# Loading the first contraction slice of b in four pieces in place of two

## The chip, the cores and the metric

The kernel runs on one core of a Trainium2 chip. The metric is the device time of one execution in microseconds, given as the median of several runs. A core has TensorE (PE, matrix products into PSUM), VectorE (DVE), ScalarE (ACT), GpSimd (POOL) and SyncE (SP), which here only issues transfers. Transfers between the device memory and the on-chip memory are carried out by 16 DMA engines; SP and POOL issue them from queues of their own.

## The reference

With a of 1024 x 1024, b of 1024 x 2048 and c of 2048 x 1024, all float32:

```python
def reference(a, b, c):
    h = np.matmul(a, b)
    h = 0.5 * h * (1 + np.tanh(np.sqrt(2 / np.pi) * (h + 0.044715 * h ** 3)))
    return np.matmul(h, c).astype(np.float32)
```

## The kernel before, in words

The kernel computes h transposed, applies the activation while it moves h out of PSUM, and multiplies by c. Both products use seven half-size block products in place of eight for part of the work (class `Seven`, function `seven`): the columns 1024 to 2047 of the first product, and the whole of the second product. The columns 0 to 1023 of the first product are done plainly, in the stretch that the change touches.

**The first stage.** The contraction of the first product has 1024 rows, cut into eight slices of 128 (KT = 8, KH = 4). For the first half of the rows of a (512 rows) and slices 0 to 3, the inputs come as float32 through staging buffers: `sta` for a, `stb` for b (columns 0 to 1023 of each slice). SP issues these loads in the order written (lines 76 to 83): slice 0 of a, slice 0 of b, slice 1 of a, slice 1 of b, slices 2 and 3 of a in one, slice 2 of b, slice 3 of b. `load_a` (L71) and `load_b` (L74) issue one transfer each.

For every slice `turn0` casts a to bf16 (VectorE, L118), transposes it on TensorE (L122) into PSUM, and copies it to `aT` (VectorE, L124). For b, ScalarE casts columns 0 to 511 (L135) and VectorE columns 512 to 1023 (L136) into `b1`. For slice 0 ScalarE's cast is cut in two of 256 columns, in the kernel before already. Then seven matmuls of 128 x 512 (L128), one per tile of 128 columns of b and each into its own PSUM bank, accumulate slice k. The first two tiles need columns 0 to 255 of the slice, the next two 256 to 511, the last three 512 and up. Eight matmuls on zeros (L89) run while the first loads are on their way.

**What follows.** POOL issues all other loads; these convert float32 to bf16 on the way. They stand behind one small copy, the gate (L85), which reads slice 1 of b in `stb` and so waits for its landing. After the gate come four loads of a (L98, the second half of its rows), slices 4 to 7 of b (L105), two more loads of a, the rest of b (L109) and c (L112). After slice 3, TensorE transposes the second half of a's rows (`turn`, L158) from what L98 loaded. The order on each engine is that of the code, since the schedule is written by hand.

**Completion of transfers.** SP's transfers rotate over eight completion semaphores: the ninth uses that of the first again, and its issue waits until the first has landed. In the kernel before SP issues eight loads and then sixteen stores of the output (L353).

These are the lines that cast b in the first stage:

```python
    for k in range(KH):
        for c0 in (0, 256) if k == 0 else (0,):
            w = 256 if k == 0 else H
            nc.scalar.activation(b1[:, k, ds(c0, w)], stb[:, k, ds(c0, w)], AF.Copy)
        nc.vector.tensor_copy(b1[:, k, H:], stb[:, k, H:])
```

Of the kernel before, what the change touches and what calls it, by code (L numbers as in the profile page):

```python
# [19 lines left out]
def kernel(ctx, tc, a, b, c, out):  # L20
# [4 lines left out]
    H = 512  # L25
# [44 lines left out]
    def load_a(k, n):  # L70
        nc.sync.dma_start(out=slice_a(k, n), in_=av[:, 0:4, ds(k * 128, n * 128)])  # L71

    def load_b(k, c0=0, w=1024):
        nc.sync.dma_start(out=stb[:, k, ds(c0, w)], in_=bv[:, k, ds(c0, w)])  # L74

    load_a(0, 1)
    load_b(0, 0, H)
    load_b(0, H, H)
    load_a(1, 1)
    load_b(1)  # L80
    load_a(2, 2)
# [330 lines left out]
```

## Time and profile before

| | |
|---|---|
| median of 8 runs | 122.38 us |
| lowest and highest | 121.48 and 124.96 us |
| the profiled execution | 121.48 us |
| its span in the profile | 119.7 us |
| TensorE busy | 112.4 us, 94% of the span |
| VectorE busy | 88.6 us, 74% |
| ScalarE busy | 50.8 us, 42% |
| bytes read and written | 20.97 MB and 4.19 MB |

The span is the time between the first and the last event of the profile; what the device time has beyond it, 1.8 us here, lies around it. The profile shows one execution. Times in it are microseconds from the start of the span. Engine names end in q where the sequencer of an engine is meant, as in SPq for SP's issues. A group of instructions is given by its line and engine, what it writes and reads, its shapes and its count, followed by its busy time, the mean length of one, and the idle time of the engine in front of it with what ended that idle time. In the list of waits the numbers after a pair are the microseconds in total, how often it occurred, and the longest.

### The profile page before, as it was taken

How to read it: one execution, taken by the hardware profiler on the slowest of the kernel's cores; microseconds unless marked ns; L12 is line 12 of the kernel's file. 1: busy time of each engine (PE TensorE's matmuls, PEld its weight loads, DVE VectorE, ACT ScalarE, POOL GpSimd, SP SyncE). 2: the span in 40 equal slices, each digit the busy share in tenths (PEclk: the TensorE clock that was granted, in tenths of full speed). 3: DMA queues.
4: the chain of work that ended last, by engine and by line, in shares of the span. 5: the costliest groups of instructions: out<-in, count | busy, mean ns of one | idle time of the engine just before them, and what ended most of it. 6: DMA issues, size and time to landing. Idle time of an engine off the chain costs nothing.

```text
span 119.7 us, 1429 instructions
## 1 busy us (share of the span) xinstructions
PE 112.4 (94%) x530; PEld 72.2 (60%) x536; DVE 88.6 (74%) x97; ACT 50.8 (42%) x82; POOL 16.3 (14%) x29
## 2 busy tenths in 40 slices
PE   6788899999999999999999999999999999999970
PEld 2234454645544445888887444468888888888850
DVE  0224488496438899987779999969999996892480
ACT  4022471007457789946769436900023595100000
POOL 2008908842242000000000000000000000000000
PEclk9999999999999999999999999999999999999999
DMA  3799999999999999998000000072000002004695
GB/s 95 175 364 394 177 169 213 206 202 206 206 207 212 210 213 212 209 210 159 8 0 0 0 5 0 0 263 88 0 0 0 0 5 88 0 0 175 246 351 192
DMA packets 11110, 16.34 MB, mean 136 GB/s; under 512 B 736, under 2 KB 5856, under 8 KB 11104
## 3 DMA queue, kind: packets, MB, share of 16 engines
q0 software_dynamic: 6496, 8.91, 42.5%
q1 hardware_dynamic: 4608, 7.34, 17.5%
q8 instruction: 4, 0.07, 0.2%
q14 instruction: 2, 0.02, 0.0%
HBM read 20.97 MB, written 4.19 MB: 210 GB/s over the span
## 4 chain that ended last, share of the span: by engine, by line
PE 78%; DMA 9%; DVE 7%; issue 1%; ACT 1%; SPq 0%; DVEq 0%; ACTq 0%
PE ps L229 51%; PE ps L128 25%; DMA out_dram<-ot 5%; DMA stb<-in_b_dram 4%; DVE x L187 4%; PE pt L158 2%; DVE ot L273 2%; PE pt L122 1%; DVE aT L124 1%; DVE ot L358 1%; ACT u L268 1%; ACT b L135 0%; SPq L71 0%; DVEq L273 0%; DVEq L358 0%
## 5 line engine op out<-in xcount | busy, mean ns | idle before, releaser
L128 PE MATMUL ps<-aT,b 128*128 128x512 bf16 x125 | 30.1, 393 | 2.0 <-DVE aT L124 1.0
L229 PE MATMUL ps<-x,s 128*128 128x512 f32 x128 | 29.6, 391 | 0.0
L229 PEld LDWEIGHTS ps<-x,s 128*128 128x128 f32 x128 | 24.0, 188 | 5.1
L128 PEld LDWEIGHTS <-b 128*128 128x128 bf16 x128 | 12.5, 100 | 16.5 <-ACT b L135 2.2
L229 PE MATMUL ps<-x,x 128*128 128x512 f32 x64 | 14.8, 389 | 0.0
L229 PE MATMUL ps<-c_sb,hT 128*128 128x512 bf16 x62 | 13.9, 379 | 0.1
L229 PEld LDWEIGHTS ps<-x,x 128*128 128x128 f32 x64 | 12.0, 188 | 2.5
L268 ACT ACTIVATE v<-ps 128x512 f32<-128x512 f32 x8 | 4.8, 599 | 17.1 <-PE ps L229 17.1
L163 ACT ACTIVATE hT<-ps 128x512 bf16<-128x512 f32 x12 | 6.8, 594 | 11.3 <-PE ps L128 11.3
L229 PE MATMUL ps<-x 128*128 128x512 f32 x48 | 11.3, 393 | 0.0
L229 PEld LDWEIGHTS <-hT 128*128 128x128 bf16 x64 | 6.2, 98 | 7.6 <-issue 0.3
L229 PEld LDWEIGHTS ps<-x 128*128 128x128 f32 x48 | 9.0, 188 | 2.0
L187 DVE TENSOR_TENSOR x<-c_sb 128x1024 fp32r<-128x1024 bf16 x8 | 9.2, 1216 | 0.0
L273 DVE TENSOR_TENSOR ot<-ps,v 128x512 f32<-128x512 f32 x8 | 5.3, 686 | 4.6 <-DMA out_dram<-ot 3.8
L258 DVE TENSOR_TENSOR half<-ps,half 128x512 f32<-128x512 f32 x8 | 5.5, 692 | 3.2 <-PE ps L128 2.9
L273 DVE TENSOR_TENSOR ot<-ps,u 128x512 f32<-128x512 f32 x8 | 5.4, 690 | 3.0 <-ACT u L268 3.0
L160 DVE COPY aT<-pt 128x1024 bf16<-128x1024 bf16 x6 | 4.0, 688 | 4.7 <-PE pt L158 4.7
L163 ACT ACTIVATE hT<-ot 128x512 bf16<-128x512 f32 x12 | 6.9, 624 | 1.1 <-DVE ot L273 1.1
L112 POOL DMA_DIRECT2D c_sb<-in_c_dram x8 | 5.7, 714 | 10.0 <-DMA b<-in_b_dram 9.1
L229 PE MATMUL ps<-aT,b 128*128 128x512 bf16 x31 | 7.0, 379 | 0.1
L268 ACT ACTIVATE p<-ps 128x512 f32<-128x512 f32 x8 | 4.7, 594 | 4.8 <-PE ps L229 4.8
L135 ACT ACTIVATE b<-stb 128x512 bf16<-128x512 f32 (+1 forms) x5 | 2.6, 541 | 9.2 <-DMA stb<-in_b_dram 9.2
(45 smaller groups left out, 115.1 us busy)
## 6 DMA issues: line engine op xcount, KB each, us to landing
c_sb<-in_c_dram POOLq DMA_DIRECT2D x8, 512.0 KB, 19.7
out_dram<-ot SPq DMA_DIRECT2D x16, 256.0 KB, 2.1
b<-in_b_dram POOLq DMA_DIRECT2D x4, 512.0 KB, 12.8
stb<-in_b_dram SPq DMA_DIRECT2D x3, 512.0 KB, 8.4
a<-in_a_dram POOLq DMA_DIRECT2D x6, 256.0 KB, 7.3
b<-in_b_dram POOLq DMA_DIRECT2D x4, 256.0 KB, 9.0
sta<-in_a_dram SPq DMA_DIRECT2D x2, 256.0 KB, 4.3
stb<-in_b_dram SPq DMA_DIRECT2D x2, 256.0 KB, 5.0
```

Source lines behind the costliest of these rows:

```text
L112: nc.gpsimd.dma_start(out=c_sb[:, t:t + 2], in_=cv[:, t:t + 2])
L122: nc.tensor.transpose(pt[:, i, ts(j, 128)], ab[:, j, ts(i, 128)], ident)
L128: nc.tensor.matmul(p, b1[:, k, ts(t, 128)], aT[:, h, k], start=(k == k0), stop=(k == k1 - 1))
L135: nc.scalar.activation(b1[:, k, ds(c0, w)], stb[:, k, ds(c0, w)], AF.Copy)
L158: nc.tensor.transpose(pt[:, n, ts(j, 128)], sts[j // 2][:, j % 2, ts((k + n) % KH, 128)], ident)
L160: nc.vector.tensor_copy(aT[:, h, k:k + 2], pt)
L163: nc.scalar.activation(hT[h][:, t], p, AF.Gelu_apprx_tanh)
L187: nc.vector.tensor_tensor(out=dst[:, r], in0=x[:, r], in1=y[:, r], op=op)
L229: nc.tensor.matmul(p[:, ds(c0, w)], l[:, k, ts(j, 128)], r[:, k, ds(c0, w)], start=(start and k == 0), stop=(k == self.kt - 1), skip_group ...
L258: nc.vector.tensor_tensor(out=half[:, t], in0=p, in1=half[:, t], op=ADD)
L268: nc.scalar.activation(st, p, AF.Copy)
L273: nc.vector.tensor_tensor(out=ot, in0=p, in1=st, op=ADD)
```

## The change

The first slice of b, 128 rows by 1024 columns of float32, is loaded by four transfers of 256 columns each. Before, it was two of 512. Nothing else in the text of the kernel changes; the casts that read the slice are the same.

```diff
     load_a(0, 1)
-    load_b(0, 0, H)
-    load_b(0, H, H)
+    for c0 in range(0, 1024, 256):
+        load_b(0, c0, 256)
     load_a(1, 1)
     load_b(1)
     load_a(2, 2)
```

SP now issues ten loads ahead of its stores, and each transfer of slice 0 moves rows of 1024 bytes where it moved rows of 2048. ScalarE's two casts of slice 0 each wait for a transfer of their own, where both waited for the first; VectorE's cast of columns 512 to 1023 waits for two transfers in place of one. On SP the issue of slice 2 of b now waits for the semaphore of slice 0 of a, and that of slice 3 for the first piece of slice 0 of b.

## The prediction

> **What bounds the kernel now.** I read the chain that ended last first, in order of time, because the change sits in the first five microseconds and the question is whether they are on the path. Columns: start us, length us, what.
>
> ```profile
> 1.22 4.66 DMA stb<-in_b_dram
> 5.90 0.43 ACT b L135
> 6.37 3.17 PE ps L128 x7
> 9.54 0.44 PE pt L122 x4
> 10.01 0.44 DVE aT L124
> 10.48 1.67 PE ps L128 x7
> ...
> 16.30 0.11 PE pt L158 x2
> 16.41 0.01 issue
> 16.42 0.51 PE pt L158 x6
> ```
>
> The first piece of b, issued at 1.22, lands at 5.88 and holds the first real matmul until 6.37. From there TensorE or what feeds it is on the path to 101.4. But the first matmul has another condition. The timeline of 4 to 7 us and the groups by shape (6 to 10 us, then 10 to 16 us) show it:
>
> ```profile
> 5.55 0.42 DVE L124 COPY aT<-pt 128x512 bf16<-128x512 bf16 x1 [1.65 <-PE pt L122]
> 5.90 0.72 ACT L135 ACTIVATE b<-stb 128x256 bf16<-128x256 f32 x2 [3.67 <-DMA stb<-in_b_dram]
> ```
> ```profile
> L128 PE MATMUL ps<-aT,b 128*128 128x512 bf16 x7 | 3.2, 630 | 0.9 <-ACT b L135 0.9
> L128 PE MATMUL ps<-aT,b 128*128 128x512 bf16 x20 | 4.8, 378 | 1.1 <-DVE aT L124 1.0
> ```
>
> aT is written at 5.97-5.99, so whatever b does, the first matmul can't start before about 6.03: 0.34 us of 6.37. And the first seven matmuls run at 630 ns (0.43 us apart), later ones at 378 (0.21 apart), although the granted clock reads 1.00.
>
> Then the list of waits between 6 and 17 us, and the same stretch in windows (PE, PEld, DVE, ACT, POOL busy, clock, DMA share, GB/s):
>
> ```profile
> ACT b L135 <- DMA stb<-in_b_dram: 9.2, 4, 3.7
> POOL gate L85 <- DMA stb<-in_b_dram: 8.1, 1, 8.1
> PEld L158 <- DMA a<-in_a_dram: 0.2, 1, 0.2
> ```
> ```profile
> 2.00:3.00 1.00, 1.00 (x4) 0.43 (x3) 0.00 (x0) 0.22 (x2) 0.00 (x0) 1.00 0.88 271
> 3.50:5.00 1.50, 1.35 (x6) 0.25 (x4) 0.40 (x1) 0.00 (x0) 0.00 (x0) 1.00 0.38 67
> 6.00:8.00 2.00, 1.63 (x4) 0.54 (x5) 0.43 (x1) 0.62 (x2) 0.00 (x0) 1.00 1.04 359
> 10.00:12.00 2.00, 1.52 (x8) 0.78 (x9) 1.46 (x3) 0.04 (x1) 2.00 (x4) 1.00 1.01 392
> ```
>
> Two things are to be seen. The small wait of 0.2 us at L158 is the second checkpoint: TensorE arrives at 16.30 and cannot go on past 16.41 until the second POOL load of a has landed (16.38). That load is issued behind the gate, which waits for b's slice 1 (landed 9.39), and shares 16 busy DMA engines. So an earlier first matmul is worth nothing at the end unless this landing comes earlier too; a later landing costs in full. After it I found no load nearer than 1.1 us to its user (b's slice 7 lands at 25.02, its first matmul comes at about 26.1). Second, the DMA engines have a hole, 67 GB/s between 3.5 and 5.0, just after b is first touched; from 6 on they are full.
>
> **What the Trainium skill says.** *DMA: Bandwidth & Descriptors*, "Issuing engines are not separate DMA queues": all transfers share the same 16 engines; "HWDGE ordering" adds that each engine takes its descriptors in ring order. The trace agrees: SP's loads land in their order, 3.45, 5.88, 7.17, 8.04, 9.39, 10.83, 12.10, 13.36. The same page, "Why small descriptors are slow", gives a fixed cost of some 3 cycles a packet; the trace's packet records have 84 ns for 2048 bytes and 46 for 1024, so 8 ns lost per split, which agrees. *TensorE: Matmul & The Clock Gate*, Part 1: the array runs at half rate until a free-running window of about 3.4 us has been busy, and the moment varies from run to run. The 630 against 378 ns agree; the varying moment can't be seen in one trace.
>
> **The change, step by step**, against the profiled execution's own 121.48 us (span 119.7 and 1.8 outside it). The median of the runs is 122.38, 0.9 above it; I carry differences over.
>
> 1. SP issues two more loads. The issue timeline:
> ```profile
> 1.22 0.97 SPq L74 DMA_DIRECT2D stb<-in_b_dram  x2
> 2.23 0.43 SPq L71 DMA_DIRECT2D sta<-in_a_dram  x1
> 2.70 0.50 SPq L74 DMA_DIRECT2D stb<-in_b_dram  x1
> ```
> An issue is 0.48 us, so the four pieces go out at 1.22, 1.70, 2.19, 2.67, and all that follows on SP (a1, b1, a2, b2, b3) goes out 0.97 later: a1 at 3.20, b1 3.67, a2 4.2, b2 4.7, b3 5.6. From the issue of the first load (0.74) to its first packet (1.84) the trace has 1.1 us, so a1 could start at 4.3. In the trace its first packets move at 5.5 and it lands at 8.04. The delay is hidden by the queue ahead of it, cover about 1.2 us; without the cover it costs up to 0.97. POOL's queue is untouched, apart from its gate.
> 2. New waits on SP. The program rotates eight completion semaphores; with ten loads, b2 now waits for a0's landing (3.45, before its issue, nothing) and b3 for the first piece (at most 5.9, against its own issue at 5.6, so 0.3 at most). Behind b3 on SP stand only the stores, the first of them after 68 us. b3's packets move after 11 us. Cost nothing. The stores keep their distance of eight.
> 3. Packets. Each engine carries 32 of 46 ns in place of 16 of 84: 1.47 against 1.34, +0.13 us of DMA work, in front of everything that lands later, so the gate and the POOL load at the checkpoint move by +0.13.
> 4. First piece. Half the bytes: 8 x 46 = 0.37 us per engine in place of 0.67, so 0.3 earlier if the hole stays where it is; how the hole falls on it the trace can't say. Bounds: 4.5 (no hole) to 5.9 (all of it). I take 5.4. ACT 0.43 later, 5.85, TensorE is held by aT: first matmul at 6.03, -0.34 (0 if it lands at 5.9).
> 5. VectorE's cast of columns 512 up (L136) now waits for two landings, 7.17 + 0.13, done 7.75; its weights are wanted at 6.03 + 4 x 0.43 = 7.75. Cost 0 to 0.1. ACT's second half waits for its own piece, wanted at 6.89; hidden unless that lands after 6.4.
> 6. Going on: transposes of slice 1 at 9.26 (9.54 before), aT at 10.17; ACT on b1 from 9.54, done 10.17, matmuls at 10.20 (10.48). Slice 2: transposes 11.87, aT 12.80, but ACT on b2 runs 12.25-12.88, matmuls at 12.93 (13.12). TensorE is thus 0.19 early, and reaches the checkpoint at 16.11. The load lands at 16.51 instead of 16.38, and TensorE goes on at 16.55 instead of 16.42.
>
> Sum: -0.34 at the first matmul, eaten on the way; +0.13 at the checkpoint: 121.6 in the profile's terms, 122.5 in the median's. The hole in the DMA could move by itself: below nothing if smaller pieces fill it (up to 1.0 us of the 1.5 are idle), above if more transfers widen it. And in the typical run, 0.9 longer than the profiled one, TensorE may be later than the load, and then the 0.2 to 0.3 us survive. Between +0.13 and -0.3 I take no change, **122.4**.
>
> **The rivals.**
>
> *Slower: the later issues are not hidden.* If b's pieces go through without the hole, or the engines must wait for each transfer's descriptors, a1, b1, a2, b2, b3 begin by their issue times, 0.97 later, and with them the gate and the checkpoint load. For it: several DMA engines stand idle between 3.6 and 5.0 us although the second half was issued by 2.19. Against: 1.2 us of queue ahead of a1. It decides once the queue ahead of a1 is under 0.97 us at its issue. Time: 122.38 + 0.97 = 123.35; half of it, 122.9.
>
> *Faster: TensorE's full rate comes earlier in the typical run.* The idle gap before the first matmul shrinks from 0.86 to 0.52 us; if that brings the clock release forward, seven matmuls at half rate cost 7 x 0.21 = 1.5 less, of which the loads leave about 0.9, the median falling to what the profiled run already is: 121.5. Against: the profiled run ran all of slice 0 at half rate and yet is the shortest, so in such a run nothing more is to be had.
>
> *The DMA hole closes.* The transfers come up to 1.0 us earlier; TensorE's own chain then caps the gain at 0.34: 122.0. This stays within the unmeasurable.
>
> *Nothing happens at the first matmul*, since the first piece takes the whole hole and lands at 5.9: then only +0.13, 122.5.
>
> **How the numbers follow.** About 0.5% (0.6 us) is what a measurement of this kernel can tell from no change. My forecast with the last two rivals, all between 121.8 and 123.0: 0.51. Faster beyond that: 0.26, the clock rival with some cases where both clock and hole move. Slower: 0.23, the issue rival and a widened hole. The range reaches to the clock rival's 121.5 and a little further and to 123.2, most of the issue rival, so that a tenth lies outside at either end.
>
> **What would show it.** SP's issues: a1 near 3.2. The landing of the first b piece: before 5.5, with the first matmul at 6.03 behind aT, shows step 4 right; at 5.9, wrong. The second POOL load of a at L158: landing 16.4 to 16.6 with a wait of 0.4 us in front of it shows steps 3 and 6 right. Wrong would be: a1 landing near 9 with DMA engines idle before it (issue rival); a landing at L158 well before 16.3 (hole closed); or matmuls of slice 0 at 378 ns (clock rival).

## The result

The changed kernel takes 123.82 us in the median of 11 runs (122.84 to 124.7; a twelfth on record took 122.6); the kernel before, 122.33 over 32 runs. The ratio is 1.0133, with a 95% interval of 1.0103 to 1.0162: slower by 1.3%, about 1.5 us. Ratios leave out executions more than 1.5% above the fastest of their kernel; both kernels have such. Run again on another occasion, in four executions, the change gave 1.0156 (1.0087 to 1.0225). The forecast of no change was wrong, and its range ended at 123.2.

The profiled execution took 123.76 us, with a span of 122.0. Its chain of waits, in order of time (start, length, what), to be held against the chain of before:

```profile
3.18 0.43 SPq L71
...
3.65 6.74 DMA stb<-in_b_dram
...
10.42 0.64 ACT b L135
...
11.10 2.56 PE ps L128 x7
13.66 0.87 PE pt L122 x8
...
15.03 2.59 PE ps L128 x11
...
18.27 0.45 PE pt L158 x8
```

The chain no longer goes through the first piece of b, but through slice 1 of b: issued at 3.65 (2.70 before), landed at 10.40 (9.39 before). Slice 1's matmuls begin at 11.10 in place of 10.48, and then last 2.56 in place of 1.67 us.

The timeline of TensorE in the changed kernel shows that slice 0 had gone the other way:

```profile
5.83 1.74 PE L128 MATMUL ps<-aT,b 128*128 128x512 bf16 x7 [0.51 <-ACT b L135]
7.46 0.40 PE L122 MATMUL pt<-ident,ab 128*128 128x128 bf16 x4
11.10 2.56 PE L128 MATMUL ps<-aT,b 128*128 128x512 bf16 x7 [3.25 <-ACT b L135]
```

The first matmul comes 0.54 us earlier and in this execution at full rate. TensorE is through with slice 0 and the transposes by 7.86, and then idles for 3.25 us. The gain of the first stage is there, and is wiped out by the wait that follows.

The windows of the changed kernel (length, then busy time of PE, PEld, DVE, ACT, POOL, granted clock, DMA share, GB/s):

```profile
3.50:5.00 1.50, 1.35 (x6) 0.25 (x4) 0.35 (x1) 0.42 (x1) 0.00 (x0) 1.00 0.72 195
6.00:8.50 2.50, 1.85 (x11) 0.63 (x9) 1.28 (x3) 0.00 (x0) 0.00 (x0) 1.00 0.81 215
12.00:15.00 3.00, 2.52 (x12) 1.35 (x11) 1.34 (x3) 1.20 (x2) 3.00 (x6) 0.50 0.97 187
```

The kernel before has 362 GB/s in the second of these windows:

```profile
6.00:8.50 2.50, 2.13 (x6) 0.71 (x7) 0.85 (x2) 0.62 (x2) 0.00 (x0) 1.00 1.04 362
```

Two things have changed. The hole in the DMA traffic, which stood between 3.5 and 5.0 us at 67 GB/s, is shallower there (195) but there is a second one from 6.0 to 8.5, while slice 1 of b is on its way. And between 12 and 15 us TensorE's granted clock is 0.50, which lengthens the matmuls of slice 1 and the transposes behind them. TensorE comes to the transposes of L158 at 18.27, where it came at 16.30 before and went on, after a short wait, at 16.42; from there on the order of its work is the same.

A third thing has changed at the other end of the kernel. This is the issue of SP's last store, first in the kernel before, then in the changed one:

```profile
116.81 0.33 SPq L353 DMA_DIRECT2D out_dram<-ot  x1
```
```profile
118.67 0.33 SPq L353 DMA_DIRECT2D out_dram<-ot  x1
```

The stores land at 118.83 and 120.73, and the spans end at 119.71 and 121.99. From the last landing to the end it is thus 0.89 us before and 1.25 us after the change. The trace shows the reason. At its end SP waits for the completion semaphores one after the other, in a fixed order and 0.06 us apart. With 24 transfers the rotation puts the last store on the semaphore that comes last in this order; with 26 it puts it on an earlier one, and six more waits follow its landing. In the twenty profiles of this case this rest goes by the number of loads from SP and ScalarE alone: 0.89 to 0.90 us with eight, 1.25 to 1.26 with ten, 1.32 with nine, 0.95 or 0.96 with seven. So 0.36 us of the loss have nothing to do with the head of the kernel; no run changed this end alone.

### The profile page after: what moved, and what is told of

The parts are those of the page before. It is cut to its first block, busy times and chain, and to the rows that moved or that the text cites. A ratio compares the mean times of both kernels' runs of the same rounds, so it can differ in the third digit from the quotient of the medians.

```text
span 122.0 us, 1432 instructions
## 1 busy us (share of the span) xinstructions
PE 111.8 (92%) x530; PEld 72.0 (59%) x536; DVE 89.0 (73%) x97; ACT 50.9 (42%) x82; POOL 16.5 (14%) x29
## 3 DMA queue, kind: packets, MB, share of 16 engines
q0 software_dynamic: 6496, 8.91, 41.9%
## 4 chain that ended last, share of the span: by engine, by line
PE 75%; DMA 11%; DVE 6%; SPq 2%; issue 1%; ACT 1%; DVEq 0%; ACTq 0%
PE ps L229 50%; PE ps L128 22%; DMA stb<-in_b_dram 6%; DMA out_dram<-ot 5%; DVE x L187 4%; PE pt L158 2%; DVE ot L273 2%; SPq L74 1%; PE pt L122 1%; SPq L71 1%; DVE ot L358 1%; ACT b L135 1%; ACT u L268 0%; DVE aT L124 0%; DVEq L273 0%
## 5 line engine op out<-in xcount | busy, mean ns | idle before, releaser
L128 PE MATMUL ps<-aT,b 128*128 128x512 bf16 x125 | 29.6, 388 | 4.4 <-ACT b L135 3.8
L229 PE MATMUL ps<-aT,b 128*128 128x512 bf16 x31 | 7.0, 379 | 0.1
```

Source lines behind the costliest of these rows:

```text
L128: nc.tensor.matmul(p, b1[:, k, ts(t, 128)], aT[:, h, k], start=(k == k0), stop=(k == k1 - 1))
L229: nc.tensor.matmul(p[:, ds(c0, w)], l[:, k, ts(j, 128)], r[:, k, ds(c0, w)], start=(start and k == 0), stop=(k == self.kt - 1), skip_group ...
```

## The experiments

Theory 1: the loss comes from the later issues on SP. Everything behind slice 0 of b is issued 0.95 us later and lands later. Theory 2: it comes from the smaller pieces, which upset the transfers. Beside these, the half rate of TensorE between 12 and 15 us: cause, or part, or nothing. The 0.36 us at the end are in every kernel here that has ten loads.

### Issues without pieces: two tiny loads

The tile `tiny` is allocated further up.

```diff
     load_b(0, 0, H)
     load_b(0, H, H)
+    for i in range(2):
+        nc.sync.dma_start(out=tiny[:, ds(4 * i, 4)], in_=bv[:, 0, ds(4 * i, 4)])
```

> b's slice 0 stays in two loads of 512 columns; two loads of 16 bytes a row stand behind them on SP, so that only the number of issues is that of the change (the tiny tile is read by nothing). Theory 1, later issues: slice 1 of a is issued near 3.2 us in place of 2.2, slice 1 of b near 3.65, it lands near 10.4 (9.4 before), and most of the loss of the change comes back: +1.0 us or more, ratio 1.008 to 1.014. Theory 2, the smaller pieces themselves: no loss, ratio 1.000 to 1.003, slice 1 of b lands near 9.4 to 9.6 though it is issued later.

Ratio 1.0112 (1.0041 to 1.0182). SP's issues in the timeline of this kernel, and the gate, which starts 0.05 after the landing of slice 1:

```profile
2.23 0.91 SPq L81 DMA_DIRECT2D tiny<-in_b_dram  x2
3.17 0.43 SPq L72 DMA_DIRECT2D sta<-in_a_dram  x1
3.65 0.51 SPq L75 DMA_DIRECT2D stb<-in_b_dram  x1
```
```profile
10.88 0.44 POOL L88 COPY gate<-stb 128x1 f32<-128x1 f32 x1 [9.59 <-DMA stb<-in_b_dram]
```

Slice 1 of b is issued at 3.65, as after the change, and lands at 10.83, later still, though slice 0 comes in two pieces. Two issues that carry 16 bytes a row cost most of what the change costs. This is with the 0.36 us at the end, and with a mean granted clock of 0.977 to 0.983 in all its four executions.

### Pieces without issues: two of the four on ScalarE's queue

`load_b` takes the issuing engine as a further argument here.

```diff
     for c0 in range(0, 1024, 256):
-        load_b(0, c0, 256)
+        load_b(0, c0, 256, nc.sync if c0 < H else nc.scalar)
```

> The four pieces of the change, with the last two issued by ScalarE at the start of its program, so that SP issues what it issued before. Theory 1: slice 1 of b is issued near 2.7 and lands near 9.4; the loss of the change goes, ratio 0.995 to 1.003. Theory 2: it lands near 10.4 as after the change, ratio 1.008 to 1.014.

Ratio 0.9978 (0.9946 to 1.0011). SP's issue timeline and the gate:

```profile
2.26 0.43 SPq L71 DMA_DIRECT2D sta<-in_a_dram  x1
2.74 0.51 SPq L74 DMA_DIRECT2D stb<-in_b_dram  x1
```
```profile
9.32 0.18 POOL L85 COPY gate<-stb 128x1 f32<-128x1 f32 x1 [8.02 <-DMA stb<-in_b_dram]
```

Ten loads, four small pieces, and no loss, although the end has its 0.36 us here too: slice 1 of b is issued at 2.74 and lands at 9.27. The order of the loads is another one as well: the two pieces on ScalarE's queue go out at 0.74 and 1.19, slice 0 of a lands at 5.42 (3.45 before), and the first matmul comes at 6.84. With this reserve the two experiments together speak for theory 1 and against theory 2 as the main cause.

### Time alone: SP held

What counts could be the clock time of the issues, or the two more transfers in SP's queue.

```diff
     load_b(0, 0, H)
     load_b(0, H, H)
+    nc.vector.memset(sta[:, ds(H, 1920)], 0.0)
     load_a(1, 1)
```

> The kernel before, with no transfer added or cut: SP is held ahead of the issue of slice 1 of a until VectorE has cleared the part of the staging buffer that it writes, to about 2.9 to 3.2 us in place of 2.2. Theory 1a, the time of issue is what counts: all landings behind come 0.7 to 1.0 us later (slice 1 of b near 10.1 to 10.4), ratio 1.006 to 1.014. Theory 1b, it is the two more transfers in SP's queue and not the clock time of the issues: slice 1 of b lands near 9.4, ratio 0.998 to 1.003.

Ratio 1.0062 (1.0031 to 1.0093). SP's timeline, the gate, and the window of the second hole:

```profile
3.17 0.38 SPq L71 DMA_DIRECT2D sta<-in_a_dram  x1
3.59 0.51 SPq L74 DMA_DIRECT2D stb<-in_b_dram  x1
```
```profile
10.96 0.44 POOL L86 COPY gate<-stb 128x1 f32<-128x1 f32 x1 [9.66 <-DMA stb<-in_b_dram]
```
```profile
6.00:8.50 2.50, 2.46 (x6) 0.89 (x7) 0.85 (x2) 0.29 (x1) 0.00 (x0) 1.00 0.89 184
```

The same eight loads with the same sizes, only 0.9 us later from slice 1 of a on: slice 1 of b lands at 10.90, and the second hole is there, 184 GB/s. The delay alone makes the late landing. It makes only half of the loss in time; with its eight loads this kernel does not have the 0.36 us at the end.

### Is the early landing of before the rule?

The profile of before was that of the shortest execution of its first eight. Three more profiles of it and one of the changed kernel, on one chip:

> The kernel before, looked at again. Theory 1a rests on slice 1 of b landing near 9.4 in one profiled execution, the shortest of its set; 256 and 768 columns landed it at 9.55 and at 10.35 with the same issue times. If the earlier landing is the rule, it lies within 9.2 to 9.7; if the issue time only shifts the odds between an early and a late landing, one or two of the three looks show 10.0 or later.

> As the look before it: slice 1 of b at 9.2 to 9.7 if the early landing is the rule, at 10.0 or later in some looks if the issue time shifts the odds.

> The third look at the kernel before: again 9.2 to 9.7 if the early landing is the rule, 10.0 or later in some looks if the issue time shifts the odds.

> The changed kernel, looked at beside the three of the kernel before: slice 1 of b lands at 10.3 to 10.8 again, as in all four executions seen so far.

The kernel before took 121.88, 121.71 and 121.68 us; slice 1 of b landed at 9.23, 9.14 and 9.28. The changed kernel took 122.97 and landed it at 10.52. With the profiles shown first (9.39 and 10.40) and a third of the changed kernel (10.49, below) the shift is 1.0 to 1.4 us in every pair. It belongs to every execution profiled, not to one. In this profile of the changed kernel TensorE ran slice 0 at half rate as in the first profile of before, and slice 1 at full rate:

```profile
6.04 3.14 PE L128 MATMUL ps<-aT,b 128*128 128x512 bf16 x7 [0.52 <-DVE aT L124]
11.23 1.68 PE L128 MATMUL ps<-aT,b 128*128 128x512 bf16 x7 [1.62 <-ACT b L135]
14.21 3.18 PE L128 MATMUL ps<-aT,b 128*128 128x512 bf16 x13 [0.52 <-DVE aT L124]
17.23 0.68 PE L158 MATMUL pt<-ident,a 128*128 128x128 bf16 x8
```

Without the half rate in slice 1 it is 1.1 to 1.3 us longer than the three beside it (one execution each). Of this, 0.36 us lie at the end. Behind the transposes of L158 TensorE goes on with its matmuls at 17.75, against 16.93 to 17.10 in the three: in these executions the late landings by themselves cost these 0.65 to 0.82 us. Slices 2 and 3 of a, whose transposes follow, landed at 12.00, against 10.6 to 10.7 in the three. In the first of those TensorE comes to L158 at 15.80 and waits there for the second POOL load of a, which sets the end as the prediction read it from the trace of before:

```profile
15.80 0.27 PE L158 MATMUL pt<-ident,a 128*128 128x128 bf16 x2
16.75 0.51 PE L158 MATMUL pt<-ident,a 128*128 128x128 bf16 x6 [0.68 <-DMA a<-in_a_dram]
```

In the changed kernel's execution beside it both conditions are met almost at once: TensorE comes at 17.23, and the second POOL load, behind its later gate, lands at 17.36.

### The half rate

> The changed kernel again, as the measure for the others of this group. Theory 1a: slice 1 of b is issued near 3.65 and lands near 10.4 again; ratio 1.010 to 1.016. If that landing was an accident of one execution, it lands near 9.5 this time.

The changed kernel again: 123.94 us, ratio 1.0156, slice 1 of b at 10.49, half rate from 11.9 to 15.4.

```diff
         if k < 2:
             turn0(k + 1, k + 1)
+        if k == 0:
+            fill = bank(7, name="fill")
+            for _ in range(10):
+                nc.tensor.matmul(fill, warm[:, 0:128], warm, start=True, stop=True)
```

> The change, with ten matmuls on zeros behind the transposes of slice 1, while TensorE waits for slice 1 of b. Their results are read by nothing. Theory 1 says nothing of the clock: slice 1 of b lands near 10.4 as after the change. If TensorE's half rate between 11.7 and 15.3 us is a part of the loss, the granted clock reads 1.0 there, the seven matmuls of slice 1 take 1.7 in place of 2.6 us, and the ratio falls to 1.005 to 1.009. If the clock is without effect: ratio 1.012 to 1.015 as after the change.

> The changed kernel with four matmuls on zeros (read by nothing) behind the transposes of slice 1. If half rate in the gap before slice 1 is a part of the loss, the time lies 0.3 to 0.7 us under that of the changed kernel of this group, ratio 1.004 to 1.010; if the clock has no part in it, within 0.2 us of it. Slice 1 of b lands near 10.4 in either case.

With ten fills, as in the lines above: ratio 1.0068 (1.0031 to 1.0104), slice 1 of b at 10.35 as expected. The interval touches that of the change, which begins at 1.0103. The 14 of 20 executions that are in the ratio all have a granted clock of 0.99 or more over their span; of the six left out, at 124.1 to 125.9 us, five have 0.985 or 0.986. Its profile, though, is of an execution with slice 0 at half rate, where the fills themselves delayed slice 1:

```profile
6.03 3.15 PE L128 MATMUL ps<-aT,b 128*128 128x512 bf16 x7 [0.51 <-DVE aT L124]
10.17 2.32 PE L144 MATMUL fill<-warm 128*128 128x512 bf16 x10 [0.52 <-DVE aT L124]
12.32 1.68 PE L128 MATMUL ps<-aT,b 128*128 128x512 bf16 x7
```

With four fills nothing was gained, 1.0148 (1.0044 to 1.0253). Four were too few to hold the rate, so this kernel doesn't test the question:

```profile
8.57 1.02 PE L144 MATMUL fill<-warm 128*128 128x512 bf16 x4 [0.52 <-DVE aT L124]
11.46 2.87 PE L128 MATMUL ps<-aT,b 128*128 128x512 bf16 x7 [1.87 <-ACT b L135]
```

The unaltered kernels give a second reading. Of 14 executions of the changed kernel that are in the ratios, 9 have a mean granted clock under 0.988 and a median of 123.95 us; the other 5 have 123.17. Of 112 of the kernel before, 8 lie under 0.988, with 123.0, and 104 above, with 122.2. So a low clock goes with some 0.8 us in either kernel, and the changed kernel has it much more often. Two reserves belong to this. The same split gives 1.0 us with two pieces on ScalarE's queue and 0.7 with SP held, but nothing with 256 and 768 columns or with a on ScalarE's queue (both below). And the record of the clock begins only when full rate is first granted: at 9.96 us in the first profile of before, at 4.94 in that of the changed kernel. Half rate ahead of this moment is not in the mean, so the executions above 0.988 are not free of it: eleven of the thirteen that were profiled ran slice 0 at half rate.

When the rate is lost again can be read from the traces. After the first grant the clock changes only in steps of 3.41 us. In seven profiles a step at full rate is followed by one at half rate while matmuls are still to come; in it TensorE was busy for 0.42 to 1.58 of the 3.41 us. In all other steps at full rate ahead of the last matmuls, some 600 in the twenty profiles, it was busy for 1.72 us or more, about half of the step, and full rate went on. These are the windows of such a step in the first and in the second profile of the changed kernel:

```profile
8.35:11.77 3.42, 0.67 (x4) 0.32 (x5) 0.43 (x1) 0.63 (x1) 1.32 (x3) 1.00 1.03 386
```
```profile
10.04:13.46 3.42, 2.06 (x14) 0.99 (x15) 1.39 (x3) 0.80 (x2) 2.88 (x5) 1.00 0.98 321
```

In the first, granted full rate early, the wait for slice 1 of b fills most of a step, and half rate follows at 11.77. In the second, granted it at 10.04, no step has so much idle time. With four fills the step has 1.36 busy us, still too few. So it is the share of busy time in a step that goes with the loss, and with it the moment of the first grant. This is read from the profiles without an exception; no run changed the idle time alone.

### Other numbers of loads

```diff
-    load_b(0, 0, H)
-    load_b(0, H, H)
+    load_b(0, 0, 256)
+    load_b(0, 256, 256)
+    load_b(0, H, H)
```

> Three pieces, of 256, 256 and 512 columns: one issue more than before. Theory 1: half the loss, slice 1 of b issued near 3.2 and landing near 9.9, ratio 1.003 to 1.008. If a loss comes only with the fourth piece: 0.998 to 1.002.

Ratio 1.0105 (1.0041 to 1.0169), more than half of the loss, and not by the expected way: in the one profile (122.97 us) slice 1 of b was issued at 3.18 and landed at 8.95, earlier than before. There the loss came at the second checkpoint, as the list of waits from 14 to 19 us has it:

```profile
PEld L159 <- DMA a<-in_a_dram: 1.5, 1, 1.5
```

The second POOL load of a landed at 17.40 in place of 16.4 to 16.7. Why it was late in that execution stays open. With nine loads the end takes 0.43 us more than before, which is a third of this loss.

```diff
-    load_b(0, 0, H)
-    load_b(0, H, H)
+    load_b(0, 0, 256)
+    load_b(0, 256, 768)
```

> Two loads again, but of 256 and 768 columns, so no issue is added. Theory 1: slice 1 of b lands near 9.4 as before; the ratio is 0.997 to 1.002, since the second load of a at L158 still holds the end. Theory 2, a small first piece upsets the transfers behind it: slice 1 of b lands near 10.4, ratio 1.008 to 1.014.

> 256 and 768 columns again, since three of its four executions were disturbed the first time. Theory 1a: no issue is added, slice 1 of b lands near 9.4 to 9.6, ratio 0.997 to 1.003. If a small first piece does harm by itself: 1.006 to 1.014.

> 256 and 768 columns, a third look. Slice 1 of b landed at 9.55 and at 10.35 with the issue times of before. Theory 1a alone gives 9.2 to 9.6. 10 or later again would mean that a small first piece delays the landings by itself, and that the added issues are not the only cause of the loss.

The first set of four executions, three of them at 125.3 to 125.6 us, gives no ratio. The second gave 1.0054 (1.0020 to 1.0088). In the three profiles, the first of them of an execution of 125.45 us, slice 1 of b landed at 9.55, 10.35 and 10.00, though it was issued at 2.7. A small first piece with a large second one therefore costs something without any added issue, about 0.6 us (0.2 to 1.1 by the interval); theory 1 doesn't account for that.

```diff
-    load_b(0, 0, H)
-    load_b(0, H, H)
+    load_b(0)
```

> One load of 1024 columns for slice 0 of b: one issue less than before, slice 1 of b issued near 2.2. Theory 1a with the floor that the bytes set (9.2 us with the loads of a on ScalarE's queue): slice 1 of b lands between 8.9 and 9.5, no later than before; the first matmul waits until about 7.1, and the ratio is 0.997 to 1.005. If few, large loads were what speeds up the landings beyond the time of issue: slice 1 of b lands by 8.6, ratio under 0.997.

> One load of 1024 columns for slice 0 of b, again. Its first look (an execution of 122.4 us, while most of its runs took 121.4 to 122.0) had slice 1 of b at 10.33, against the 8.9 to 9.5 that theory 1a gives for an issue at 2.2. If that look was untypical: 8.9 to 9.5 now. If landings go by something else than the issue times: 10 or later again. Ratio 0.993 to 0.999 in either case.

One load is faster than the kernel before: 0.9959 (0.9929 to 0.9990), and 0.9964 (0.9941 to 0.9987) in a second set, by 0.4%. In the first profile slice 1 of b landed at 10.33 against the expectation, in the second at 8.91, in line with it. The chain of the second has no transfer in it at all up to 17.7 us:

```profile
1.19 3.61 PE warmps L88 x8
...
6.04 3.17 PE ps L127 x7
...
10.14 1.67 PE ps L127 x7
...
15.96 0.45 PE pt L157 x8
```

The whole slice landed at 5.54, before the second half of the kernel before did (6.6 to 7.2), and the first matmul waits only for aT. This version beats both kernels.

### Two other orders

```diff
-        nc.sync.dma_start(out=slice_a(k, n), in_=av[:, 0:4, ds(k * 128, n * 128)])
+        nc.scalar.dma_start(out=slice_a(k, n), in_=av[:, 0:4, ds(k * 128, n * 128)])
```

> The kernel before, with the three loads of a issued by ScalarE at the start of its program, so that SP issues slice 1 of b near 1.7 in place of 2.7 us. Theory 1a: landings follow the issues as far as the engines can carry the bytes; slice 1 of b lands by 8.6 to 9.0, and the second load of a at L158 with it; ratio 0.990 to 0.998. If the landings are held by the bytes alone, slice 1 of b lands at 9.3 or later and the ratio is 0.998 to 1.006.

Ratio 1.0091 (1.0068 to 1.0114). Slice 1 of b, issued at 1.66, landed at 9.17, no earlier than before; slice 0 of a, now sharing the DMA engines with b from the start, landed at 6.04 (3.45 before), and slices 2 and 3 of a at 12.90 (10.83). An issue a microsecond earlier brought nothing here; that the bytes ahead then hold the landing is the likely reading (387 GB/s from 6.0 to 8.5 us, no hole), but with a on another queue the order of those bytes changed too.

```diff
-    load_a(1, 1)
-    load_b(1)
+    load_b(1)
+    load_a(1, 1)
```

> The change, with slice 1 of b issued ahead of slice 1 of a, near 3.2 in place of 3.65 us. Theory 1a: slice 1 of b lands near 9.9, its gate opens 0.5 earlier than after the change; slice 1 of a lands later, by 8.5 to 9.5, which the transposes can bear; ratio 1.004 to 1.011. If the time of issue is not what counts: as after the change, 1.011 to 1.016.

On top of the change: 1.0104 (0.9986 to 1.0221), which settles nothing; in the one profile, of an execution of 125.68 us, slice 1 of b landed at 9.42, slice 1 of a only at 10.37, and that now held TensorE.

## Why the prediction was wrong

**Step 1, the later issues, failed.** Their times were right: slice 1 of a at 3.18 (3.20 forecast), slice 1 of b at 3.65 (3.67). That the delay is "hidden by the queue ahead of it, cover about 1.2 us" was wrong. The cover was worked out from the first load, 1.1 us from issue to first packet, and from slice 1 of a alone. Slice 1 of a did come through, at 6.95, 8.18 and 8.32 in three profiles against 7.4 to 8.0 in the four of before. It was the next load that paid: slice 1 of b takes 6.4 to 6.7 us from issue to landing in the kernel before and 6.7 to 6.9 in the changed one, so that 0.95 us of later issue became 1.0 to 1.4 us of later landing. Holding SP alone moved the landing by 1.5 to 1.8. Half the delay did not: issued at 3.18, slice 1 of b landed at 8.95 with three pieces, and at 9.42 with four where slice 1 of a stood behind it. Slices 2 and 3 of a and slice 2 of b follow at 11.88 and 13.15 in place of 10.83 and 12.10, again 1.05 later.

**Step 2, the waits on SP, was right at the head and wrong at the end.** Slices 2 and 3 of b were issued at 4.68 and 5.23, without a wait to be seen. But the step put the stores behind them at nothing, since they "keep their distance of eight". They do; the two more loads move the last store to another semaphore, and that costs 0.36 us.

**Step 3, packets, +0.13 us,** is not to be seen on its own beside 1 us. The 8 ns lost per split agree with the three cycles cited there in kind, not in size: by the step's own figures 32 bytes take about 1.2 ns (38 ns for 1024 bytes), so that three cycles, at the 32 bytes a cycle of the example in the section that it cites, would be an estimated 3.6 ns, less than half of what was measured.

**Step 4, the first piece, was right and useless.** It landed at 4.38 (4.41 and 3.99 in the two other profiles), below the lower bound of 4.5 and 1 us before the 5.4 taken; the first matmul came at 5.83, 6.04 and 5.90 (6.03 forecast). Note that in one of the four profiles of the kernel before it came at 6.07 as well. Step 5 cost nothing: the last piece landed at 6.17, ahead of the 7.30 reckoned with.

**Step 6 failed with step 1.** TensorE was to come to the checkpoint at L158 at 16.11 and to wait there until 16.55. It comes at 18.27 in the first profile, with the load there since 17.14, and at 17.23 in the profile without half rate in slice 1, with the load landing at 17.36. The wait that was to set the end is gone or next to nothing: the way to it has become as long or longer.

**The rivals.** The slower one named the mechanism, "the later issues are not hidden", with a chance of 0.23 and a price of 0.97 us. The price is about right for the landings, which cost 0.65 to 0.82 us. It looked for the sign in the wrong place (slice 1 of a near 9), and left out the end, with 0.36 us, and the half rate, which goes with 123.9 in place of 123.2. That its 123.35 comes near the 123.82 measured is therefore in part luck. The clock was a rival in the prediction only as a gain: that full rate may come earlier. It did, at 5 us in two of the three profiles of the changed kernel, and was lost again in the longer idle time, just where TensorE had become the path. The kernel before has an early grant in one profile too, at 5.75:

```profile
6.42 1.68 PE L128 MATMUL ps<-aT,b 128*128 128x512 bf16 x7 [0.90 <-ACT b L135]
9.85 1.69 PE L128 MATMUL ps<-aT,b 128*128 128x512 bf16 x7 [1.52 <-ACT b L135]
```

It gained nothing: 121.71 us, beside 121.88 and 121.68 with slice 0 at half rate, since TensorE then waits for slice 1 of b.

**The sum, and what is open.** As an estimate from the figures above: of the 1.6 us that the ratio of 1.0133 means, 0.36 lie at the end; a low clock in 9 of 14 executions in place of 8 of 112, at 0.8 us each, makes some 0.45; about 0.8 are left for the late landings, for which the profile without half rate in slice 1 has 0.65 to 0.82. SP held costs 0.6%, some 0.76 us, with a low clock in 5 of 14 executions and nothing at the end. The parts fit the whole, but only the delay was changed alone.

Why the landing is so late is open. The trace shows single engines falling behind: in the first profile of the changed kernel fifteen of the 16 are done with slice 1 of b between 8.1 and 9.5 us and one at 10.4, and the landing waits for it; before, they are done between 8.1 and 9.4. The second hole is no mark of late issues: from 6.0 to 8.5 us the changed kernel has 215 to 263 GB/s in three profiles and the kernel before 319 to 362 in four, but 256 and 768 columns have 226 to 272 and one load has 239 and 262, with slice 1 of b issued at 2.7 and 2.2. Late issues bring the late landing about, as the held SP shows, but they are not the only thing that can.

## What to carry to other kernels

At the head of a kernel the issuing queue is a resource like any other: each transfer put ahead of the others moves the issue of all of them by 0.48 us here. Two of them moved the landings behind by 1 us and more, also of loads that seemed to have a queue in front of them; one, with three pieces, did not in its one profile, though that kernel lost time as well. Read the cover from the transfer that the path waits for, from its own issue to its own landing, and not from the first one. If the first data must come in smaller pieces, issue some from an idle engine (four pieces cost nothing that way), and try the other direction too: one load in place of two was 0.4% faster. And look at the end of the profile as well as at the place of the change: where transfers take completion semaphores in turn, two loads more at the head cost 0.36 us behind the last store.

## What the runs showed that was not expected

- Slice 1 of b, 512 KB and the fifth load on SP before, the seventh after, needs 6.4 to 6.9 us from issue to landing in these two kernels, nearly the same whether it is issued at 2.7 or at 3.65. Over all the kernels here it needs 5.8 to 8.1.
- Its 16 engines finish within 1.3 us of each other in the kernel before, and within 2.3 us in the changed one (8.08 to 10.40).
- Slice 0 of b as one load of 512 KB landed whole at 5.54 in one profile and at 6.75 in the other; as two of 256 KB, at 6.6 to 7.2 in four profiles.
- TensorE lost full rate after a step of 3.41 us with at most 1.58 us of busy time, and kept it with 1.72 or more, in all twenty profiles.
- The time from the last landing to the end of the span is the same within 0.01 us in all profiles with the same number of loads from SP and ScalarE.
